# Joined steps for the four tiles of an up-projection group in a one-core encoder layer

## The chip, the cores and the metric

The kernel runs on one core of a Trainium2 chip. The metric is the device time of one execution in microseconds (us); lower is better. Engines are named as in the profile: PE does matrix products, DVE is the vector engine, ACT the scalar (activation) engine, POOL and SP here mostly issue DMA transfers. Each engine runs its own instructions strictly in the order in which they were written for it, and waits at an instruction until the semaphores that it names have been raised.

## What is computed

One encoder layer on 256 positions (T) of 2048 features: a mixer block, then a gated MLP with a convolution over positions, then a final norm. The change lies in the MLP:

```
def conv_ffn(x, g_norm, w_up, conv_k, conv_b, w_down):
    h = rms_norm(x, g_norm)
    up = h @ w_up                                   # (256, 2 * 5504)
    t = up.shape[1]
    pad = jnp.pad(up, ((0, 0), (1, 1), (0, 0)))
    up = (pad[:, :t] * conv_k[0] + pad[:, 1:t + 1] * conv_k[1]
          + pad[:, 2:t + 2] * conv_k[2] + conv_b)
    gate, val = jnp.split(up, 2, axis=-1)
    return x + (jax.nn.silu(gate) * val) @ w_down
```

## The kernel before

**Numbers in two halves.** Products are made of operands that are split into a high and a low half: high times high, low times high, high times low. Weights arrive in *pieces* of 256 rows and up to 512 columns. `split_to` makes the halves of a piece: ACT writes `whi` (line 170), DVE subtracts to get `wlo` (line 171). Four buffers hold `whi` and `wlo`, five hold the raw piece `wraw`.

**The order.** Nothing is scheduled by a program: instructions go out in the order in which the Python code calls them. `begin(i)` opens piece i: it issues the load of piece i+4, then the split of piece i+3 (`split_to(i + SPLIT_AHEAD + 1)`), and then runs the steps that were put at piece i with `at(i, f)`, in the order in which they were put there. So the split of a piece stands in ACT's and DVE's queues behind all steps of the pieces opened earlier.

**The up projection** has 22 groups. A group makes two (the last one: one) tiles of 128 gate channels and as many tiles of value channels, each 128 x 256, from 8 pieces; a full group has 4 PSUM banks, the last one 2. The pieces of the last group have half the columns (128x512 in a split, against 128x1024). `spread_products` issues the high products of two pieces (line 222), then the low products of both (line 226); in a group's last two pieces the high products of the sixteenth 128-row block come behind the low ones.

**Behind a group**, `ev_up(...)` takes its results through these steps: add the two halves of each bank into `ta` (ACT line 1059, DVE line 1061); scale by the norm's factor `rb` (DVE line 1067); middle tap and bias into `tc` (ACT line 1069); the two side taps (DVE lines 1072, 1074); SiLU of the gate (ACT line 1079); gate times value (DVE line 1080); split into the halves of `a`, the left operand of the down projection (ACT line 541, DVE line 542). All but the first run while the pieces of the next group are multiplied: `conv(0)` at its second piece (1 of 0 to 7) with the first gate tile and the first value tile, `conv(1)` two pieces later with the second ones (in the group before last: four pieces later), `gate` and the split one and two pieces behind each. For 13 of the 21 pairs of `a` tiles, sums of blocks are also made (`act_blocks`, lines 323 to 326), split into a tile `so` and written to DRAM by POOL.

**Beside it**, eight jobs (`split_ahead`) load parts of the down weights early into `tw`, add (line 1291), split (ACT line 1296 into the same `so`, DVE line 1297) and write them to DRAM. Each spans two groups: two adds in the last two pieces of the first, two adds and two splits in pieces 0, 1, 2 and 4 of the second.

**The down projection** follows at once: six plain pieces first (lines 317 to 319, twelve products each, the third of them the first to need `wlo`), then pieces in other forms with sums and stored halves that POOL loads into `hpool` and into a pool `twice`. That pool takes the place of the pools of `ta`, `so` and `tw`.

Of the kernel before, what the change touches and what calls it, by code (L numbers as in the profile page):

```python
# [8 lines left out]
F32 = mybir.dt.float32  # L9
BF16 = mybir.dt.bfloat16  # L10
F32R = mybir.dt.float32r
AF = mybir.ActivationFunctionType
OP = mybir.AluOpType
# [3 lines left out]
T = 256  # L17
# [8 lines left out]
NF = DFF // 128  # L26
# [52 lines left out]
def trunk_kernel(ctx, tc, x, x_t, vecs, w_in, ln_g, ln_b, w_st, b_s, rpb, w_branch, w_out, w_up, w_down,  # L79
                 norm_final, out):  # L80
    nc = tc.nc
    ctx.enter_context(tc.manual_schedule())

    def pool(name, side="left", bufs=1, space=None):
        kw = {} if space is None else {"space": space}
        st = ExitStack()
        p = st.enter_context(tc.tile_pool(name=name, bufs=bufs, side=side, reuse_waits="tile", **kw))
        return p, st
# [11 lines left out]
    turns, turns_st = pool("turns")  # L100
    turns = {"p": turns}
# [87 lines left out]
    def at(i, f):  # L189
        tasks.setdefault(i, []).append(f)  # L190

    cur = [0]
# [128 lines left out]
    def act_blocks(w, a11, a21, a12, a22):  # L321
        s3, n1, p2, s4 = (w[:, n * 128:(n + 1) * 128] for n in range(4))
        nc.vector.tensor_sub(s3, a11, a21)
        nc.vector.tensor_sub(n1, a22, a21)
        nc.vector.tensor_add(p2, n1, a11)
        nc.vector.tensor_sub(s4, a12, p2)
# [149 lines left out]
    ck = const.tile([128, 4, 2 * NF], F32)  # L476
# [63 lines left out]
    def split_plain(p, dst):  # L540
        nc.scalar.activation(dst[:, 0, :], p, AF.Copy)
        nc.vector.tensor_sub(dst[:, 1, :], p, dst[:, 0, :].bitcast(F32))
# [26 lines left out]
    def first_room(name, dt):  # L569
        return ypool.tile([128, 2, 512], dt, name=f"y{first_rooms.index('t13' if name == 'f' else name)}")  # L570
# [405 lines left out]
    rs = {}  # L976
# [73 lines left out]
    ff = {}  # L1050

    def ev_up(f0, nb):
        def done(ps, i):
            n = nb
            a = []
            own = {}
            for p in ps:
                t = turns["p"].tile([128, T], F32, name="tb", bufs=3)
                nc.scalar.activation(t, p[:, T:], AF.Copy)
                u = turns["p"].tile([128, T], F32, name="ta", bufs=6)  # L1060
                nc.vector.tensor_add(u, p[:, :T], t)
                a.append(u)

            def conv(b):
                c = []
                for u, ch in ((a[b], f0 + b), (a[n + b], NF + f0 + b)):
                    nc.vector.tensor_mul(u, u, rs["rb"])  # L1067
                    v = ff["p"].tile([128, T], F32, name="tc", bufs=4)
                    nc.scalar.activation(v, u, AF.Identity, scale=ck[:, 1, ch:ch + 1], bias=ck[:, 3, ch:ch + 1])  # L1069
                    c.append((u, v, ch))  # L1070
                for u, v, ch in c:
                    nc.vector.scalar_tensor_tensor(v[:, 1:], u[:, :T - 1], ck[:, 0, ch:ch + 1], v[:, 1:],  # L1072
                                                   op0=OP.mult, op1=OP.add)
                    nc.vector.scalar_tensor_tensor(v[:, :T - 1], u[:, 1:], ck[:, 2, ch:ch + 1], v[:, :T - 1],
                                                   op0=OP.mult, op1=OP.add)
                at(cur[0] + 1, lambda: gate(b, c[0][1], c[1][1]))

            def gate(b, g, v):
                nc.scalar.activation(g, g, AF.Silu)
                nc.vector.tensor_mul(g, g, v)  # L1080
                at(cur[0] + 1, lambda: split_plain(g, ff["a"][f0 + b]))
                own[b] = g
                if b and f0 // 2 in ff["kept"]:
                    at(cur[0] + 2, sums)
                    at(cur[0] + 3, sums_split)

            def sums():
                own["w"] = ff["more"].tile([128, 512], F32, name="sw")
                act_blocks(own["w"], *(own[k][:, t * 128:(t + 1) * 128] for k in range(2) for t in range(2)))

            def sums_split():
                o = ff["more"].tile([128, 2, 512], F32R, name="so")
                split_plain(own["w"], o)
                nc.gpsimd.dma_start(ff["kept"][f0 // 2], o.bitcast(F32))

            at(i + 1, lambda: conv(0))
            if n > 1:
                at(i + (5 if f0 + 3 == NF else 3), lambda: conv(1))
        return done


# [124 lines left out]
    for n, (q, i, j) in enumerate(X_SUMS):  # L1226
        sum_acts_at(i, j, first_sums[2 * q], lambda q=q: q,
                    lambda name, dt, i=i: first_room("s2" if name == "f" and i < 16 else name, dt), f"s{n}", True)
# [97 lines left out]
    for n, (pair, g) in enumerate((pair, g) for g in range(2) for pair in OUT_SPLIT[g]):  # L1326
        t_kept[pair, g] = split_rows("out", pair, g)
        i = g_at[2 * n][1]
# [46 lines left out]
    for n, q in enumerate(OUT_PAIRS):  # L1375
        i = g_m2[0][1] + OUT_SUMS[n]
# [3 lines left out]
    for f in range(0, NF, 2):  # L1380
        nb = min(2, NF - f)
# [27 lines left out]
    for p, turn in zip(DOWN_SPLIT, DOWN_JOBS):  # L1409
        for g in range(2):  # L1410
            d_kept[p, g] = split_rows("down", p, g)
            i = g_up[turn[g]][1]
# [178 lines left out]
```

## Time and profile before

| | |
|---|---|
| Median of 3 runs | 1292.68 us (1291.73 to 1294.64) |
| The profiled execution | 1291.66 us, span of its instructions 1289.9 us |
| PE busy in the span | 1279.3 us (99%) |
| DVE, ACT busy | 1120.4 us (87%), 795.5 us (62%) |
| Up projection on PE | 583.71 to 1064.72 us of the span |
| A full group of it, the last group | 22.27 us, 11.17 us |

Times in a row are from the start of the span. A timeline row gives start, duration, engine, line, operation, output and inputs, how many such instructions follow each other, and the idle time of the engine before it with what ended it. Consecutive instructions of an engine overlap in part: the end of one is later than the start of the next, so what an instruction costs its queue is the distance from its start to the start of the next one, and what it costs one who waits for it is its duration.

### The profile page before, as it was taken

The numbers are of one execution on the slowest core, as the hardware profiler recorded it, in microseconds if no ns is written. First come the engines' busy times: TensorE is split into PE (matmuls) and PEld (weight loads), VectorE is DVE, ScalarE is ACT, GpSimd is POOL, SyncE is SP. The second block draws the span as 40 slices with busy tenths as digits, with TensorE's granted clock in tenths as the row PEclk, the third lists the DMA queues.
The fourth block names the chain that finished last, engine by engine and source line by source line (L and its number), as shares of the span: only waits on it lengthen the run. The fifth ranks groups of instructions, "written<-read, shape, count | busy, mean of one in ns | idle before, by whom it ended". The sixth has DMA issues, their size and how long they took to land.

```text
span 1289.9 us, 19698 instructions
## 1 busy us (share of the span) xinstructions
PE 1279.3 (99%) x6717; PEld 1088.6 (84%) x6717; DVE 1120.4 (87%) x1664; ACT 795.5 (62%) x1181; POOL 169.0 (13%) x307
## 2 busy tenths in 40 slices
PE   9999999999999999999999999999999999999997
PEld 7888888888887888888888888888888888888885
DVE  7898977777789988996889899898988989889987
ACT  7766566766655655566565666566665656655654
POOL 0003706513000001100001001100000001211210
PEclk9999999999999999999999999999999999999999
DMA  9779889899789977965588788888866859998993
GB/s 367 275 277 277 279 273 340 292 325 321 258 309 345 350 240 254 401 222 169 185 290 280 238 291 294 268 270 285 266 221 220 280 171 357 373 390 319 361 384 141
DMA packets 199893, 369.51 MB, mean 286 GB/s; under 512 B 15984, under 2 KB 124144, under 8 KB 199792
## 3 DMA queue, kind: packets, MB, share of 16 engines
q1 hardware_dynamic: 175472, 286.36, 64.8%
q0 software_dynamic: 23888, 81.23, 17.8%
q8 instruction: 52, 0.85, 0.3%
q10 hardware_dynamic: 432, 0.66, 0.1%
q14 instruction: 49, 0.40, 0.1%
HBM read 320.48 MB, written 45.61 MB: 284 GB/s over the span
## 4 chain that ended last, share of the span: by engine, by line
PE 96%; DVE 2%; DMA 1%; issue 1%; DVEq 0%; ACT 0%; SPq 0%; ACTq 0%
PE bank L222 31%; PE bank L226 16%; PE bank L319 11%; PE bank L317 11%; PE bank L318 11%; PE bank L250 5%; PE bank L252 5%; PE bank L251 5%; DVE wlo L171 1%; DMA wraw<-in_w_down_dram 1%; PE bank L867 0%; PE bank L819 0%; PE bank L857 0%; DMA xr<-in_x_t_dram 0%; PE bank L698 0%
## 5 line engine op out<-in xcount | busy, mean ns | idle before, releaser
L171 DVE TENSOR_TENSOR wlo<-wraw,whi 128x1024 fp32r<-128x1024 f32 (+1 forms) x472 | 537.8, 1152 | 124.4 <-ACT whi L170 76.8
L170 ACT ACTIVATE whi<-wraw 128x1024 fp32r<-128x1024 f32 (+1 forms) x472 | 463.6, 995 | 227.1 <-PE bank L318 65.2
L222 PE MATMUL bank<-h,whi 128*128 128x512 f32 x1760 | 423.6, 391 | 0.0
L222 PEld LDWEIGHTS bank<-h,whi 128*128 128x128 f32 x1760 | 322.7, 188 | 62.6 <-issue 0.5
L226 PEld LDWEIGHTS bank<-h,wlo 128*128 128x128 f32 x1760 | 225.9, 191 | 8.7
L226 PE MATMUL bank<-h,wlo 128*128 128x256 f32 x1760 | 228.6, 283 | 0.0
L1069 ACT ACTIVATE tc<-ta,ck 128x256 f32<-128x256 f32 x86 | 47.1, 595 | 110.0 <-DVE ta L1067 110.0
L319 PE MATMUL bank<-wlo,a 128*128 128x512 f32 x188 | 73.4, 390 | 0.2 <-DVE wlo L171 0.2
L317 PE MATMUL bank<-whi,a 128*128 128x512 f32 x188 | 73.2, 389 | 0.0
L318 PE MATMUL bank<-whi,a 128*128 128x512 f32 x188 | 73.2, 389 | 0.0
L319 PE MATMUL bank<-wlo,h 128*128 128x512 f32 x186 | 72.5, 390 | 0.1
L318 PE MATMUL bank<-whi,h 128*128 128x512 f32 x186 | 72.5, 390 | 0.0
L317 PE MATMUL bank<-whi,h 128*128 128x512 f32 x186 | 72.5, 390 | 0.0
L1072 DVE SCALAR_TENSOR_TENSOR tc<-ta,ck,tc 128x255 f32<-128x255 f32 x86 | 41.4, 482 | 14.4 <-ACT tc L1069 14.4
L250 PE MATMUL bank<-whi,y 128*128 128x512 f32 x128 | 50.4, 394 | 0.0
L250 PE MATMUL bank<-whi,h 128*128 128x512 f32 x128 | 50.3, 393 | 0.0
L252 PE MATMUL bank<-wlo,y 128*128 128x512 f32 x128 | 49.8, 389 | 0.0
L252 PE MATMUL bank<-wlo,h 128*128 128x512 f32 x128 | 49.8, 389 | 0.0
L251 PE MATMUL bank<-whi,y 128*128 128x512 f32 x128 | 49.8, 389 | 0.0
L251 PE MATMUL bank<-whi,h 128*128 128x512 f32 x128 | 49.8, 389 | 0.0
L1301 POOL DMA_DIRECT2D down_h<-so x16 | 8.7, 545 | 309.3 <-ACT so L1296 187.2
L374 ACT ACTIVATE h<-h 128x1024 fp32r<-128x1024 f32 x36 | 38.0, 1058 | 13.8 <-DVE h L364 7.1
(324 smaller groups left out, 2005.3 us busy)
## 6 DMA issues: line engine op xcount, KB each, us to landing
wraw<-in_w_up_dram SPq DMA_DIRECT2D x336, 256.0 KB, 4.1
wraw<-in_w_in_dram SPq DMA_DIRECT2D x107, 512.0 KB, 6.6
wraw<-in_w_down_dram SPq DMA_DIRECT2D x78, 512.0 KB, 7.2
wraw<-in_w_in_dram SPq DMA_DIRECT2D x70, 256.0 KB, 4.8
wraw<-in_w_branch_dram SPq DMA_DIRECT2D x32, 512.0 KB, 5.5
wraw<-in_w_out_dram SPq DMA_DIRECT2D x28, 512.0 KB, 5.9
h<-sums POOLq DMA_DIRECT2D x18, 512.0 KB, 7.5
tw<-in_w_down_dram POOLq DMA_DIRECT2D x8, 1024.0 KB, 8.6
```

Of the source, the lines that this page charges most:

```text
L170: nc.scalar.activation(h[:, k, :m], w[:, k, :m], AF.Copy)
L171: nc.vector.tensor_sub(l[:, k, :m], w[:, k, :m], h[:, k, :m].bitcast(F32))
L222: nc.tensor.matmul(p, h[:, k - k0, b * 128:(b + 1) * 128], acts(k), start=k == 0, stop=k == nk - 1)
L226: nc.tensor.matmul(p[:, :T], l[:, k - k0, b * 128:(b + 1) * 128], acts(k)[:, 0, :], start=False, stop=False)
L250: nc.tensor.matmul(p, xh, h[:, kk, :m], start=st, stop=False)
L251: nc.tensor.matmul(p, xl, h[:, kk, :m], start=False, stop=False)
L252: nc.tensor.matmul(p, xh, l[:, kk, :m], start=False, stop=sp)
L317: nc.tensor.matmul(p, xh, h, start=st, stop=False, **kw)
L318: nc.tensor.matmul(p, xl, h, start=False, stop=False, **kw)
L319: nc.tensor.matmul(p, xh, l, start=False, stop=sp, **kw)
L1069: nc.scalar.activation(v, u, AF.Identity, scale=ck[:, 1, ch:ch + 1], bias=ck[:, 3, ch:ch + 1])
L1072: nc.vector.scalar_tensor_tensor(v[:, 1:], u[:, :T - 1], ck[:, 0, ch:ch + 1], v[:, 1:], op0=OP.mult, op1=OP.add)
```

## The change

The four tiles of a group share one `ta` tile (128 x 4 x 256) and one `tc` tile, each with one buffer. Seven steps follow at pieces 1 to 7 of the next group, each in a piece of its own: scaling of all four tiles in one DVE instruction, four middle taps on ACT, eight side taps on DVE (first all left ones, then all right ones), one SiLU, one product, one copy of the high halves, one subtraction of the low halves with the block sums behind it. The split of the block sums follows one and two pieces later, in a tile `sp` of its own.

```
-            at(i + 1, lambda: conv(0))
-            if n > 1:
-                at(i + (5 if f0 + 3 == NF else 3), lambda: conv(1))
+            u = turns["p"].tile([128, 2 * nb, T], F32, name="ta", bufs=1)
+            for n, p in enumerate(ps):
+                nc.scalar.activation(u[:, n], p[:, T:], AF.Copy)
+                nc.vector.tensor_add(u[:, n], p[:, :T], u[:, n])
+            def scale():
+                rb = rs["rb"]
+                nc.vector.tensor_mul(u, u, bass.AP(tensor=rb.tensor, offset=rb.offset,
+                                                   ap=[rb.ap[0], [0, 2 * nb], [1, T]]))
+            def middle():
+                v = box["v"] = ff["p"].tile([128, 2 * nb, T], F32, name="tc", bufs=1)
+                for n, ch in enumerate(channels):
+                    nc.scalar.activation(v[:, n], u[:, n], AF.Identity, scale=ck[:, 1, ch:ch + 1],
+                                         bias=ck[:, 3, ch:ch + 1])
+            def sides():
+                v = box["v"]
+                for tap, to, of in ((0, slice(1, T), slice(0, T - 1)), (2, slice(0, T - 1), slice(1, T))):
+                    for n, ch in enumerate(channels):
+                        nc.vector.scalar_tensor_tensor(v[:, n, to], u[:, n, of], ck[:, tap, ch:ch + 1], v[:, n, to],
+                                                       op0=OP.mult, op1=OP.add)
+            def silu():
+                nc.scalar.activation(v[:, :nb], v[:, :nb], AF.Silu)
+            def gate():
+                nc.vector.tensor_mul(v[:, :nb], v[:, :nb], v[:, nb:])
+            def high():
+                nc.scalar.activation(ff["ap"][f0 // 2][:, :, 0, :], box["v"][:, :nb], AF.Copy)
+            def low():
+                nc.vector.tensor_sub(a[:, :, 1, :], v[:, :nb], a[:, :, 0, :].bitcast(F32))
...
+            def sums_high():
+                box["o"] = ff["more"].tile([128, 2, 512], F32R, name="sp")
...
+            steps = [scale, middle, sides, silu, gate, high, low]
+            if f0 // 2 in ff["kept"]:
+                steps += [sums_high, sums_low]
+            for n, step in enumerate(steps):
+                at(i + 1 + n, step)
```

What that moves is shown at the last group, whose pieces are half as wide. Its pieces are called U0 to U7 here, the first pieces of the down projection D0, D1 and so on; the splits of half a piece show as 128x2x256 below. DVE from the results of the group before last on, in the kernel before (`ta` are the added banks, `tc` the taps, `a_6118` the pair of left operands):

```order
L1061 TENSOR_TENSOR ta<-bank,tb 128x256 x4
L171 TENSOR_TENSOR wlo<-wraw,whi 128x2x256 x2
L1067 TENSOR_TENSOR ta<-ta,rb 128x256 x2
L1072 SCALAR_TENSOR_TENSOR tc<-ta,ck,tc 128x255
L1074 SCALAR_TENSOR_TENSOR tc<-ta,ck,tc 128x255
L1072 SCALAR_TENSOR_TENSOR tc<-ta,ck,tc 128x255
L1074 SCALAR_TENSOR_TENSOR tc<-ta,ck,tc 128x255
L171 TENSOR_TENSOR wlo<-wraw,whi 128x2x256
L1080 TENSOR_TENSOR tc<-tc 128x256
L171 TENSOR_TENSOR wlo<-wraw,whi 128x2x256
L542 TENSOR_TENSOR a_6118<-tc,a_6118 128x256
L171 TENSOR_TENSOR wlo<-wraw,whi 128x2x256
```

The splits are those of U3 and U4, then U5, U6 and U7; four side taps stand between U4 and U5. The same stretch of DVE's order now:

```order
L1057 TENSOR_TENSOR ta<-bank,ta 128x256 x4
L171 TENSOR_TENSOR wlo<-wraw,whi 128x2x256 x2
L1103 TENSOR_TENSOR sp<-sw,sp 128x512
L1063 TENSOR_TENSOR ta<-ta,rb 128x1024
L171 TENSOR_TENSOR wlo<-wraw,whi 128x2x256 x2
L1076 SCALAR_TENSOR_TENSOR tc<-ta,ck,tc 128x255 x8
L171 TENSOR_TENSOR wlo<-wraw,whi 128x2x256
L171 TENSOR_TENSOR wlo<-wraw,whi 128x1024
L1085 TENSOR_TENSOR tc<-tc 128x512
```

All eight side taps now stand between the split of U6 and that of U7, and the split of the block sums (line 1103), which stood ahead of the bank adds, stands behind U4's split. ACT at the same place, before:

```order
L1059 ACTIVATE tb<-bank 128x256 x4
L170 ACTIVATE whi<-wraw 128x2x256 x2
L1069 ACTIVATE tc<-ta,ck 128x256 x2
L170 ACTIVATE whi<-wraw 128x2x256
L1079 ACTIVATE tc<-tc 128x256
L170 ACTIVATE whi<-wraw 128x2x256
L541 ACTIVATE a_6118<-tc 128x256
L170 ACTIVATE whi<-wraw 128x2x256
L170 ACTIVATE whi<-wraw 128x1024
```

The last row is D0. ACT now:

```order
L1056 ACTIVATE ta<-bank 128x256 x4
L170 ACTIVATE whi<-wraw 128x2x256
L1099 ACTIVATE sp<-sw 128x512
L170 ACTIVATE whi<-wraw 128x2x256 x2
L1069 ACTIVATE tc<-ta,ck 128x256 x4
L170 ACTIVATE whi<-wraw 128x2x256 x2
L1081 ACTIVATE tc<-tc 128x512
L170 ACTIVATE whi<-wraw 128x1024 x2
```

The four middle taps stand ahead of U6's high half, and the SiLU, which waits for the side taps on DVE, stands ahead of D0's.

More of the change, by code (lines that the diff above doesn't have):

```diff
@@ L1053, in done @@
         def done(ps, i):
[L1054 to L1089, printed above, removed]
@@ L1091, in sums_split @@
-            def sums_split():
-                o = ff["more"].tile([128, 2, 512], F32R, name="so")
-                split_plain(own["w"], o)
-                nc.gpsimd.dma_start(ff["kept"][f0 // 2], o.bitcast(F32))
-            at(i + 1, lambda: conv(0))
-            if n > 1:
-                at(i + (5 if f0 + 3 == NF else 3), lambda: conv(1))
+            u = turns["p"].tile([128, 2 * nb, T], F32, name="ta", bufs=1)
+            for n, p in enumerate(ps):
+                nc.scalar.activation(u[:, n], p[:, T:], AF.Copy)
+                nc.vector.tensor_add(u[:, n], p[:, :T], u[:, n])
@@ new lines, in done @@
+            box = {}
+            channels = [f + b for f in (f0, NF + f0) for b in range(nb)]
+            def scale():
[7 more added lines that the diff above has]
+                                         bias=ck[:, 3, ch:ch + 1])
@@ new lines, in sides @@
+            def sides():
[5 more added lines that the diff above has]
+            def silu():
+                v = box["v"]
+                nc.scalar.activation(v[:, :nb], v[:, :nb], AF.Silu)
@@ new lines, in gate @@
+            def gate():
+                v = box["v"]
+                nc.vector.tensor_mul(v[:, :nb], v[:, :nb], v[:, nb:])
+            def high():
+                nc.scalar.activation(ff["ap"][f0 // 2][:, :, 0, :], box["v"][:, :nb], AF.Copy)
+            def low():
+                v, a = box["v"], ff["ap"][f0 // 2]
+                nc.vector.tensor_sub(a[:, :, 1, :], v[:, :nb], a[:, :, 0, :].bitcast(F32))
+                if f0 // 2 in ff["kept"]:
+                    box["w"] = ff["more"].tile([128, 512], F32, name="sw")
+                    act_blocks(box["w"], *(v[:, k, t * 128:(t + 1) * 128] for k in range(2) for t in range(2)))
@@ new lines, in sums_high, with sums_low @@
+            def sums_high():
+                box["o"] = ff["more"].tile([128, 2, 512], F32R, name="sp")
+                nc.scalar.activation(box["o"][:, 0], box["w"], AF.Copy)
+            def sums_low():
+                o = box["o"]
+                nc.vector.tensor_sub(o[:, 1], box["w"], o[:, 0].bitcast(F32))
+                nc.gpsimd.dma_start(ff["kept"][f0 // 2], o.bitcast(F32))
+            steps = [scale, middle, sides, silu, gate, high, low]
+            if f0 // 2 in ff["kept"]:
+                steps += [sums_high, sums_low]
```

## The prediction, made before the changed kernel had run

> **What bounds the kernel now.** I read the page's first part, then PE's waits, then the timelines of the last up-projection group, since its pieces give everybody half the time.
>
> ```profile
> PE 1279.3 (99%) x6717; PEld 1088.6 (84%) x6717; DVE 1120.4 (87%) x1664; ACT 795.5 (62%) x1181; POOL 169.0 (13%) x307
> ```
> ```profile
> PE bank L498 <- DVE one L488: 1.5, 1, 1.5
> PE bank L317 <- DVE g L604: 0.8, 1, 0.8
> PE bank L319 <- DVE wlo L171: 0.2, 1, 0.2
> ```
>
> These three waits are all that PE has, and the first two (lines 488 and 604) lie ahead of the up projection. So in the stage that the change touches PE sets the pace alone; work saved on DVE or ACT buys nothing, and the only question is whether some half of a weight now reaches PE too late. The stage by windows, one full group with a job beside it and the last group:
>
> ```profile
> 853.15:875.42 22.27, 22.27 (x129) 19.68 (x128) 20.98 (x36) 13.86 (x21) 2.70 (x5) 1.00 0.81 258
> 1053.55:1064.72 11.17, 11.17 (x66) 9.83 (x64) 9.71 (x20) 6.82 (x15) 1.01 (x2) 1.00 0.81 241
> ```
>
> After the window's length stand the busy times of PE, its weight loads, DVE, ACT and POOL, then the granted clock (1.00) and the DMA share. DVE is busy 20.98 of 22.27 us: it is no bound, but it has little room to catch up. Now PE at the end of the up projection and the start of the down projection:
>
> ```profile
> 1063.30 1.12 PE L226 MATMUL bank<-h,wlo 128*128 128x256 f32 x8
> 1064.25 0.63 PE L222 MATMUL bank<-h,whi 128*128 128x512 f32 x2
> 1064.72 0.39 PE L317 MATMUL bank<-whi,a 128*128 128x512 f32 x1
> 1064.95 0.40 PE L318 MATMUL bank<-whi,a 128*128 128x512 f32 x1
> 1065.18 0.39 PE L319 MATMUL bank<-wlo,a 128*128 128x512 f32 x1
> ```
>
> The eight low products take 0.95 us (1063.30 to 1064.25); the first four are U6's, so U7's `wlo` is due at 1063.78. D0's `whi` is due at 1064.72, its `wlo` 0.46 us later, at 1065.18. DVE before, where it met these dates:
>
> ```profile
> 1049.27 0.29 DVE L323 TENSOR_TENSOR sw<-tc 128x128 f32<-128x128 f32 x1
> ...
> 1051.92 0.69 DVE L171 TENSOR_TENSOR wlo<-wraw,whi 128x512 fp32r<-128x512 f32 x1 [1.51 <-DMA wraw<-in_w_up_dram]
> 1052.53 0.69 DVE L542 TENSOR_TENSOR so<-sw,so 128x512 fp32r<-128x512 f32 x1
> 1053.47 1.42 DVE L1061 TENSOR_TENSOR ta<-bank,tb 128x256 f32<-128x256 f32 x4 [0.26 <-ACT tb L1059]
> 1054.93 0.69 DVE L171 TENSOR_TENSOR wlo<-wraw,whi 128x512 fp32r<-128x512 f32 x1
> ...
> 1058.32 0.48 DVE L1074 SCALAR_TENSOR_TENSOR tc<-ta,ck,tc 128x255 f32<-128x255 f32 x1
> 1058.72 0.48 DVE L1072 SCALAR_TENSOR_TENSOR tc<-ta,ck,tc 128x255 f32<-128x255 f32 x1
> 1059.24 0.48 DVE L1074 SCALAR_TENSOR_TENSOR tc<-ta,ck,tc 128x255 f32<-128x255 f32 x1
> ...
> 1061.66 0.69 DVE L171 TENSOR_TENSOR wlo<-wraw,whi 128x512 fp32r<-128x512 f32 x1
> ```
>
> The last row is U7: done at 1062.35, 1.4 us before PE asks. This is the thinnest cover in the stage, and the change rearranges just this stretch.
>
> **The change, part by part.** *Fewer instructions on DVE.* One 128x1024 and one 128x512 instruction cost their queue, by the next rows (start to start), 1.13 and 0.60 us; a 128x256 one costs 0.34.
>
> ```profile
> 840.29 1.22 DVE L171 TENSOR_TENSOR wlo<-wraw,whi 128x1024 fp32r<-128x1024 f32 x1
> 841.42 0.42 DVE L1080 TENSOR_TENSOR tc<-tc 128x256 f32<-128x256 f32 x1
> 841.76 1.22 DVE L171 TENSOR_TENSOR wlo<-wraw,whi 128x1024 fp32r<-128x1024 f32 x1
> ```
> ```profile
> 853.08 0.68 DVE L1291 TENSOR_TENSOR tw<-tw 128x512 f32<-128x512 f32 x1
> 853.68 0.68 DVE L542 TENSOR_TENSOR so<-sw,so 128x512 fp32r<-128x512 f32 x1
> ```
>
> Per group the scaling falls from 4 x 0.34 = 1.36 to 1.13, product and low halves from 4 x 0.34 to 2 x 0.60: 0.39 us saved. Side taps cost 0.40 where the next is independent (1058.32 to 1058.72) and 0.52 where it needs this one's result (1058.72 to 1059.24). In the new order none needs the one just before it: eight at 0.40 = 3.2 us, against 4 x 0.92 = 3.7. Together about 0.9 us less DVE time in a group, and the waits inside `conv` go too. On PE's path all of it is worth nothing, since no wait of PE in this stage is there to remove: 0.
>
> *The order in full groups.* The side taps stand together, 3.2 us ahead of U7's kind of split. PE in the group from 853.15 on, and DVE's split of its last piece:
>
> ```profile
> 862.35 2.08 PE L226 MATMUL bank<-h,wlo 128*128 128x256 f32 x16
> ```
> ```profile
> 872.58 2.08 PE L226 MATMUL bank<-h,wlo 128*128 128x256 f32 x16
> ```
> ```profile
> 854.28 1.41 DVE L1061 TENSOR_TENSOR ta<-bank,tb 128x256 f32<-128x256 f32 x4
> ...
> 869.67 1.22 DVE L171 TENSOR_TENSOR wlo<-wraw,whi 128x1024 fp32r<-128x1024 f32 x1
> ```
>
> Piece 7's low half is due at 872.58 + 0.95 = 873.53; before, it was there at 870.89. Now: the split of piece 6 needs the buffer of piece 2, which PE frees at about 862.35 + 0.95 + 0.16 = 863.46, and its high half stands behind the four middle taps. The bank adds were over by 855.7; taken 0.5 later, since the block sums now stand just ahead of them, DVE needs from 856.2 on 2 x 1.13 for two splits, 2 x 0.60 for job adds, 0.60 for the block sums' split and 1.13 for the scaling: 861.4. Middle taps then run to 863.5 (beside piece 5's split and the job's on DVE), the high half to 864.6, the split of piece 6 to 865.8, the side taps to 869.1, the split of piece 7 to 870.3. That is 3.2 us early, a little better than before: 0 in 21 groups. If the side taps cost more than 6.4 us, this cover would be gone.
>
> *The last group.* The same order, with half the time. ACT's prices there:
>
> ```profile
> 1057.16 1.09 ACT L1069 ACTIVATE tc<-ta,ck 128x256 f32<-128x256 f32 x2 [1.75 <-DVE ta L1067]
> 1058.16 0.62 ACT L170 ACTIVATE whi<-wraw 128x512 fp32r<-128x512 f32 x1
> ...
> 1065.21 1.04 ACT L170 ACTIVATE whi<-wraw 128x1024 fp32r<-128x1024 f32 x1
> ```
>
> Two middle taps hold ACT 1.00 us, half a piece takes 0.62, a whole piece 1.04. DVE, from U2's split at 1051.92 on, which waits for PE to free a buffer and so does not move: that split 0.61; low halves of the group before (128x512) 0.60; block sums, four at 0.29 at most, 1.1; four bank adds at 0.34, 1.36; these end at 1055.6, 0.7 later than before. U3 and U4 0.61 each, split of the block sums 0.60, scaling 1.13: 1058.55, its result 0.09 later. U5: 1059.2. Meanwhile ACT's four middle taps run from 1058.65 to 1060.65 and U6's high half to 1061.25. DVE: U6 to 1061.9, eight side taps to 1065.1, U7's split (0.69 to its end) to 1065.8. Due at 1063.78: **PE waits 2.0 us.**
>
> *Is that made good later?* D0's high half stands behind the SiLU, which waits for the sixth side tap: 1061.9 + 5 x 0.40 + 0.48 = 1064.4. SiLU of 128x512 is taken as long as U6's copy of that size, 0.6; D0's high half is there at 1066.05 and its low half, 1.22 later, at 1067.3. PE, 2.0 late, asks at 1066.7 and 1067.2: 0.1 more. So even without the wait at U7 a wait of 2.1 us at D0 would stand in its place; the two are one delay, not two. D1's low half (gate product 0.60, split 1.22) is there at 1069.1, due 0.46 after D1's start, which is twelve products or 2.7 us behind D0's: 1070.0. From there on DVE leads again. PE has no idle time to give back until the end, so the sum is **+2.1 us**: 1293.8 us for the profiled execution's 1291.66. That execution is 1.0 below the median of the runs, so against the median 1292.68 + 2.1 = 1294.8 us.
>
> Bounds of that term: side taps at 0.52 each (if the semaphore and not the dependence costs the 0.12) add 1.0 us: 3.1. If the bank adds end as early as before (0.7) and block sums cost 0.2 each (0.4), 1.0. I take the middle, as each step there is a row of the same shape.
>
> [...]
>
> *POOL.* Its loads into `twice` wait for the last reader of the space, now the side taps of the last group, at D3 and not D1. Before:
>
> ```profile
> 1070.66 0.53 POOL L1391 DMA_DIRECT2D s<-sums  x1 [4.95 <-DVE ta L1061]
> 1076.09 0.53 POOL L1251 DMA_DIRECT2D h<-down_h  x1 [4.89 <-ACT whi L170]
> ```
> ```profile
> 1070.00:1075.00 5.00, 5.00 (x24) 4.13 (x23) 4.63 (x9) 3.12 (x6) 0.53 (x1) 1.00 1.03 419
> 1075.00:1080.00 5.00, 5.00 (x24) 4.14 (x23) 4.93 (x9) 3.31 (x6) 2.11 (x4) 1.00 1.02 388
> ```
>
> Following DVE on (bank adds, D3 to D6 and four sums of 0.6), those side taps end near 1081.5; five loads of 0.5 MB then take 2.6 MB / 388 GB/s = 6.8 us alone and perhaps 13 beside the weights: 1094. They are for a piece twelve behind D0 (eight plain ones of 2.7 us, two pairs of 21 products of 0.23 each, so at 1096 before and 1098 now): 0, with 4 us spare.
>
> **The rivals.** *No wait after all* (0.14): DVE or ACT run the last stretch 2 us faster than these rows; the time stays 1292.7. Against it: two separate chains, U7's and D0's, give the same delay. *The delay grows in the down projection* (0.17): transfers there have a DMA share of 1.02 and 1.03, the loads moved from 1071 to 1082 leave the queues idle first and crowd the weights after. If half the 6.8 us is lost as capacity, 3.4, and PE's own 2.1 covers its part, 1.3 more: 1296.1. It decides once those loads land past 1098. *Full groups wait too* (0.05): side taps past 6.4 us; 1 us in each of 8 groups with jobs gives 1303. *DVE is the bound after all* (0.04): the 0.39 us of joined instructions in 21 groups, 8 us, come off: 1284.5. PE's missing waits speak against it. [...]
>
> **The numbers.** The likeliest, a single delay of 1.0 to 3.1 us, has 0.60: 1294.8 us. The range takes in "no wait" and most of the growing delay: 1291.6 to 1297.6, leaving out the last two rivals and the far end of the third. About 0.2% (2.6 us) is what a measurement can tell from no change. A fifth of the likeliest lies over +2.6 (0.12), with 0.15 of the third's and 0.05: slower 0.32. Faster 0.04. Within: 0.64.
>
> **What would show it.** In the profile after: PE's waits name `wlo` of line 171 (or `whi`) once, at about 1063.8, for some 2 us, and no other up-projection piece; eight side taps of 0.40 between U6's and U7's splits; full groups still 22.27 us; DVE busy 15 to 20 us less. Wrong would be: PE without a wait at that place, full groups longer than 22.3 us, or waits on loads past 1080.

## The result, and the profile after

The changed kernel takes 1296.34 us (median of 9 runs, 1294.16 to 1297.00) against 1292.48 us for the kernel before beside it: ratio 1.0027, 95% interval 1.0019 to 1.0036. It is slower by 3.9 us, 0.3%. The profiled execution takes 1294.97 us, with a span of 1292.9 us.

First the page of the changed kernel, then PE's waits in it:

```profile
PE 1280.2 (99%) x6717; PEld 1088.4 (84%) x6717; DVE 1101.7 (85%) x1558; ACT 790.4 (61%) x1139; POOL 168.9 (13%) x307
```
```profile
PE bank L226 <- DVE wlo L171: 1.8, 1, 1.8
PE bank L498 <- DVE one L488: 1.5, 1, 1.5
PE bank L317 <- DVE g L604: 1.2, 1, 1.2
```

DVE is busy 18.7 us less (1120.4 before), and nothing of that shows in the time. One wait is new: low products (line 226) wait for `wlo`, once. The windows of a full group with a job and of the last group:

```profile
854.26:876.53 22.27, 22.27 (x129) 19.68 (x128) 20.80 (x33) 14.91 (x22) 2.65 (x5) 1.00 0.85 276
1054.66:1065.83 11.17, 10.38 (x59) 8.93 (x57) 8.98 (x21) 6.21 (x14) 1.01 (x2) 1.00 0.73 245
```

The full group is as long as before, to the hundredth. The last group, which starts 1.11 us later than before (1054.66 against 1053.55), is not finished after its 11.17 us. DVE and PE at its end, by the timeline:

```profile
1059.56 0.69 DVE L171 TENSOR_TENSOR wlo<-wraw,whi 128x512 fp32r<-128x512 f32 x1
1062.38 0.69 DVE L171 TENSOR_TENSOR wlo<-wraw,whi 128x512 fp32r<-128x512 f32 x1 [2.12 <-ACT whi L170]
1062.99 3.24 DVE L1076 SCALAR_TENSOR_TENSOR tc<-ta,ck,tc 128x255 f32<-128x255 f32 x8
1066.14 0.68 DVE L171 TENSOR_TENSOR wlo<-wraw,whi 128x512 fp32r<-128x512 f32 x1
1067.14 1.23 DVE L171 TENSOR_TENSOR wlo<-wraw,whi 128x1024 fp32r<-128x1024 f32 x1 [0.31 <-ACT whi L170]
```
```profile
1064.41 0.63 PE L226 MATMUL bank<-h,wlo 128*128 128x256 f32 x4
1066.88 0.74 PE L226 MATMUL bank<-h,wlo 128*128 128x256 f32 x4 [1.84 <-DVE wlo L171]
1067.46 0.62 PE L222 MATMUL bank<-h,whi 128*128 128x512 f32 x2
1067.92 0.39 PE L317 MATMUL bank<-whi,a 128*128 128x512 f32 x1
1068.15 0.39 PE L318 MATMUL bank<-whi,a 128*128 128x512 f32 x1
1068.42 0.50 PE L319 MATMUL bank<-wlo,a 128*128 128x512 f32 x1
```

The splits are U5, U6, U7 and D0; the eight side taps stand between U6 and U7. Four low products start 0.12 us apart, so U7's first was to start at 1064.41 + 4 x 0.12 = 1064.88; it starts at 1066.88: **2.0 us late**. The last row is D0's first use of `wlo`, 0.27 instead of 0.23 us behind its neighbour: 0.04 us more, and no second wait. Behind it PE never waits again.

The span is 3.0 us longer than that of before, and 1.1 of it lie ahead of the change, where the up projection starts later. Its first high products in the kernel before, in the changed kernel, and in a second profile of the kernel before (run later, below):

```profile
583.71 1.75 PE L222 MATMUL bank<-h,whi 128*128 128x512 f32 x7
```
```profile
584.81 0.62 PE L222 MATMUL bank<-h,whi 128*128 128x512 f32 x2
```
```profile
584.70 0.84 PE L222 MATMUL bank<-h,whi 128*128 128x512 f32 x3
```

The unchanged kernel starts there at 584.70 too. So that 1.1 us needs no change of the kernel: it is scatter between executions, and the first profile of before was a quick one.

### The profile page after: what moved, and what is told of

Same layout as the page of the kernel before. It is cut to its first block, busy times and chain, and to the rows that moved or that the text cites. A ratio compares the mean times of both kernels' runs of the same rounds, so it can differ in the third digit from the quotient of the medians.

```text
span 1292.9 us, 19590 instructions
## 1 busy us (share of the span) xinstructions
PE 1280.2 (99%) x6717; PEld 1088.4 (84%) x6717; DVE 1101.7 (85%) x1558; ACT 790.4 (61%) x1139; POOL 168.9 (13%) x307
## 4 chain that ended last, share of the span: by engine, by line
PE 96%; DVE 2%; DMA 1%; issue 0%; ACT 0%; DVEq 0%; ACTq 0%
PE bank L222 31%; PE bank L226 16%; PE bank L319 11%; PE bank L317 11%; PE bank L318 11%; PE bank L250 5%; PE bank L252 4%; PE bank L251 4%; DMA wraw<-in_w_in_dram 1%; DVE wlo L171 1%; PE bank L867 0%; PE bank L819 0%; PE bank L857 0%; DMA xr<-in_x_t_dram 0%; PE bank L698 0%
## 5 line engine op out<-in xcount | busy, mean ns | idle before, releaser
L1076 DVE SCALAR_TENSOR_TENSOR tc<-ta,ck,tc 128x255 f32<-128x255 f32 x172 | 69.8, 480 | 0.0
L785 POOL TENSOR_SCALAR_AFFINE_SELECT bias<-run 64x128 f32<-64x128 f32 x64 | 36.6, 605 | 81.2 <-DVE sc L827 80.6
```

What stands on the lines that cost most here:

```text
L1076: nc.vector.scalar_tensor_tensor(v[:, n, to], u[:, n, of], ck[:, tap, ch:ch + 1], v[:, n, to], op0=OP.mult, op1=OP.add)
```

## The experiments

"Joined" means the steps as the change writes them, "spread" those of before.

**The changed kernel again** (no edit).

> The changed kernel once more, as the yardstick of the other three. Theory A (one delay: U7's low half behind eight side taps, D0's high half behind the SiLU): the trace shows one PE wait in the up projection, 2.0 us before the low products of U7, and the time is 2 us over before (ratio 1.0016). Rival B (joined steps cost a second thing that this wait does not hold, for instance the later POOL loads into `twice` or the full groups): 3 to 5 us over before again (1.0023 to 1.0039), with 1 to 3 us that no PE wait in the last group explains.

Measured: 1295.57 us (8 runs, 1294.56 to 1297.19) against 1292.17; ratio 1.0028, interval 1.0017 to 1.0038. The loss is real, 3.4 us this time. Its profile has the same 2.0 us wait, and one thing more, which the last section shows.

**Spread steps only behind the group before last**, joined ones in the other twenty-one.

```
-            for n, step in enumerate(steps):
-                at(i + 1 + n, step)
+            if f0 + 3 != NF:
+                for n, step in enumerate(steps):
+                    at(i + 1 + n, step)
+                return
...
+            at(i + 1, lambda: conv(0))
+            at(i + 5, lambda: conv(1))
```

> Joined steps in every group but the one before last, whose two pairs of tiles go through the old steps in the old pieces (on the shared tiles); POOL's loads into `twice` still wait for the side taps of the last group. Theory A: no PE wait over 0.3 us after line 604's; ratio 1.000 within its interval; U7's low half 1.0 to 1.5 us early. Rival B: the rest of the loss stays, 1 to 3 us over before (1.0008 to 1.0023).

Measured: 1293.42 us; ratio 1.0010, 1.0001 to 1.0019. The wait at U7 is gone, and two thirds of the loss with it. A smaller one stands at D1, in PE's timeline of this kernel:

```profile
1068.45 0.39 PE L318 MATMUL bank<-whi,a 128*128 128x512 f32 x1
1069.39 0.50 PE L319 MATMUL bank<-wlo,a 128*128 128x512 f32 x1 [0.56 <-DVE wlo L171]
```

D1's `wlo` comes 0.94 instead of 0.23 us behind: 0.7 us. The group ahead of it still has joined steps, so the split of its block sums (0.60 us on DVE) still stands behind the bank adds. PE's waits on `wlo` in this run count one more: at 1274.88, near the end of the down projection, a product comes 0.66 us late, where the kernel before has 0.36.

**The reverse: joined steps only behind the group before last**, spread ones elsewhere, with the block sums' split at its old place.

```
-            for n, step in enumerate(steps):
-                at(i + 1 + n, step)
+            if f0 + 3 == NF:
+                for n, step in enumerate(steps):
+                    at(i + 1 + n, step)
+                return
...
```

> The opposite: old steps in the old pieces in every group (on the shared tiles), joined steps only behind the group before last. The split of the block sums stands ahead of the bank adds again, so DVE comes to the scaling 1.3 us earlier than in the changed kernel. Theory A: one PE wait before U7's low products, 2.0 - 1.3 = 0.7 to 0.8 us, and a time 0.8 us over before (ratio 1.0006). Rival B (the loss comes from the 20 other groups): no more than 0.3 us. A rival C (the joined order in the last group is harmless, its length does it): 2 us.

Measured: 1294.30 us; ratio 1.0015, 1.0007 to 1.0024. The wait is back at U7, from these steps alone, though smaller:

```profile
1063.80 0.63 PE L226 MATMUL bank<-h,wlo 128*128 128x256 f32 x4
1065.62 0.74 PE L226 MATMUL bank<-h,wlo 128*128 128x256 f32 x4 [1.18 <-DVE wlo L171]
```

1065.62 - (1063.80 + 0.48) = 1.34 us; I had expected 0.7 to 0.8. So of the 2.0 us, 1.34 come from the joined steps of this one group; by difference, 0.66 come from the joined steps of the group ahead of it, which put the block sums and their split later. I had taken off the whole 1.3 us that these cost DVE. About half of that is lost, because DVE, so much earlier here, waits before U4's split until PE frees a buffer:

```profile
1056.61 0.69 DVE L171 TENSOR_TENSOR wlo<-wraw,whi 128x512 fp32r<-128x512 f32 x1 [0.53 <-PE bank L226]
```

The time is 2.1 us over before, 0.8 more than the wait; that part stays open.

**The joined steps of the group before last three pieces later.**

```
-                at(i + 1 + n, step)
+                at(i + (4 if f0 + 3 == NF else 1) + n, step)
```

> The changed kernel with the seven joined steps of the group before last three pieces later (scaling at U4, side taps at U6, SiLU at U7, product at D0, and so on); no other edit and no less work. Theory A: now the splits of U7, D0 and D1 stand ahead of the side taps and those of D2 on behind, where pieces last 2.7 us; no PE wait over 0.3 us, D2's low half 0.7 us early, ratio 1.000. Rival B: 1 to 3 us over before (1.0008 to 1.0023). If the amount of joined work in the last group counted and not what it stands ahead of, it would wait 2 us as before.

Measured: 1294.24 us; ratio 1.0017, 1.0008 to 1.0026. No wait at U7 or from D0 to D6; but one at D7, which I had not expected:

```profile
1083.05 0.39 PE L318 MATMUL bank<-whi,a 128*128 128x512 f32 x1
1084.70 0.50 PE L319 MATMUL bank<-wlo,a 128*128 128x512 f32 x1 [1.26 <-DVE wlo L171]
```

It is 1.65 - 0.23 = 1.4 us long. DVE in that kernel shows why:

```profile
1078.71 0.69 DVE L171 TENSOR_TENSOR wlo<-wraw,whi 128x512 fp32r<-128x512 f32 x1 [1.74 <-ACT whi L170]
1079.32 0.69 DVE L363 TENSOR_TENSOR h<-wraw 128x512 f32<-128x512 f32 x1
...
1081.85 1.66 DVE L1076 SCALAR_TENSOR_TENSOR tc<-ta,ck,tc 128x255 f32<-128x255 f32 x4
1083.43 1.22 DVE L171 TENSOR_TENSOR wlo<-wraw,whi 128x1024 fp32r<-128x1024 f32 x1
```

Steps moved out of one full stretch of DVE's queue pushed the next one: the last group's side taps and four weight sums now end just when D7's split is due.

**No side taps behind the group before last.**

```
             def sides():
                 v = box["v"]
+                if f0 + 3 == NF:
+                    return
```

> The changed kernel without the eight side taps of the group before last (its gate values are computed without them; 3.2 us of VectorE work, nothing else). Theory A (the whole loss is PE waiting at U7 for the split behind these taps): U7's `wlo` is ready 3.2 us earlier, so the 2.0 us wait is gone, none stands in its place at D0 to D7, and the time is that of before, ratio 0.9990 to 1.0010. Theory B (part of the loss is elsewhere: the timed 3.1 to 3.9 us are more than the 2.0 us wait): the waits are gone and 1 to 2 us remain, ratio 1.0008 to 1.0016.

Measured: 1292.35 us against 1292.40; ratio 0.9998, 0.9989 to 1.0007. Theory A. With 3.2 us of DVE work out of one place, no other change undone, all of the loss is gone, so it hangs on this one wait; twenty groups of joined steps cost and save nothing that this interval (some 1.2 us to each side) can show. DVE's splits of U6 and U7 now follow each other, and U7's is done at 1063.94:

```profile
1062.65 1.29 DVE L171 TENSOR_TENSOR wlo<-wraw,whi 128x512 fp32r<-128x512 f32 x2 [2.13 <-ACT whi L170]
```

**Later steps again, with the last group's side taps ahead of the weight sums.**

```
                 v = box["v"] = ff["p"].tile([128, 2 * nb, T], F32,
-                    name="tc", bufs=1)
+                    name="tc" if nb > 1 else "tl", bufs=1)
...
+            if nb == 1:
+                steps[:2] = [lambda: (scale(), middle())]
             for n, step in enumerate(steps):
-                at(i + 1 + n, step)
+                at(i + (4 if f0 + 3 == NF else 1) + n, step)
```

> The changed kernel with the group before last started three pieces later, as in the run before this one, and the last group's scaling and middle taps in one step, so that its side taps come a piece earlier and stand ahead of the weight sums, not between them and D7's split (its middle taps get a tile of their own). Theory A (position in VectorE's queue decides): no wait at U7, D0 to D2, nor at D7 (1.65 us before): no PE wait in this stage, ratio 0.9990 to 1.0008. Rival (the VectorE work itself is too much for this stretch wherever it stands): a wait of 0.5 to 1.5 us appears at another down piece, ratio 1.0008 to 1.0018.

Measured: 1294.43 us; ratio 1.0015, 1.0006 to 1.0024. Theory A's forecast of no wait fails: D7 waits 1.8 us, not less than before. The rows of ACT and DVE of this kernel:

```profile
1074.71 1.09 ACT L1069 ACTIVATE tl<-ta,ck 128x256 f32<-128x256 f32 x2 [1.10 <-DVE ta L1063]
1075.71 1.56 ACT L170 ACTIVATE whi<-wraw 128x1024 fp32r<-128x1024 f32 x2
```
```profile
1076.79 1.23 DVE L171 TENSOR_TENSOR wlo<-wraw,whi 128x1024 fp32r<-128x1024 f32 x1 [2.12 <-ACT whi L170]
```

The middle taps, a piece earlier, now stand ahead of a high half on ACT (1075.71), and DVE, which stands at that piece's split, waits 2.1 us with the side taps behind it. I had moved the work past DVE's obstacle and into ACT's. The rival, too much work wherever it stands, forecast another piece and a ratio of 1.0008 to 1.0018. The ratio lies there, but the wait is at D7 as before and DVE had 2.1 us idle, so the amount of its work is not the reason.

**How long is the cover in a full group?** Two runs, with 8 and with 16 further side taps (3.2 and 6.4 us) in three groups that are not neighbours, whose gate values change by them; the factor 2 is 3 in the second. In the first profile after, where no job stands ahead, DVE's split of a group's last piece (the first of two here) and the low products that need it:

```profile
847.26 2.36 DVE L171 TENSOR_TENSOR wlo<-wraw,whi 128x1024 fp32r<-128x1024 f32 x2
```
```profile
851.42 2.08 PE L226 MATMUL bank<-h,wlo 128*128 128x256 f32 x16
```

It is ready at 847.26 + 1.22 = 848.48 and due 0.95 behind the second row's start, at 852.37: a cover of 3.9 us.

```
-                for tap, to, of in ((0, ...), (2, ...)):
+                for tap, to, of in ((0, ...), (2, ...)) * (2 if f0 in (20, 28, 36) else 1):
```

> The changed kernel with eight further side taps (3.2 us of VectorE; the gate values of these groups change) in three full groups that are not neighbours. In the trace of the changed kernel piece 7's low half is ready 3.9 us ahead of PE in such groups. Theory A (cover): 3.2 is less than 3.9, so PE does not wait and these groups still take 22.27 us. Rival (VectorE's busy time counts): each of the three groups becomes longer by up to 3.2 us less its idle 2.4 to 2.9 us, 0.3 to 0.8 each.

> The same with sixteen further side taps (6.4 us of VectorE) in the same three groups. Theory A (cover): PE waits 6.4 - 3.9 = 2.5 us for `wlo` once in each of the three groups, 7.5 us in all, besides the 2.0 us at U7. Rival (buffers further ahead make it good): no wait, or under 1 us in each. Rival (busy time counts): 6.4 - 2.4 to 2.9 = 3.5 to 4.0 us in each.

Measured with 8 (one run of each): 1294.87 us, and no wait in the up projection but the one at U7. With 16: 1303.12 us, and one wait in each of the three groups. PE's waits of that kernel, and the first of them:

```profile
PE bank L226 <- DVE wlo L171: 8.9, 4, 2.4
```
```profile
851.74 0.28 PE L226 MATMUL bank<-h,wlo 128*128 128x256 f32 x1
854.34 0.86 PE L226 MATMUL bank<-h,wlo 128*128 128x256 f32 x5 [2.32 <-DVE wlo L171]
```

2.60 us between two starts that are otherwise 0.12 apart: 2.5 us, as the cover of 3.9 us said (6.4 - 3.9), and nothing at 3.2. By busy time it would have been 3.5 to 4.0 us in each group, and 0.3 to 0.8 with 8. In such a group the distance of one split from its date decides.

**Spread steps behind the group before last, and the block sums a piece earlier.**

```
             if f0 // 2 in ff["kept"]:
                 steps += [sums_high, sums_low]
+            if f0 + 5 == NF:
+                steps[4:6] = [lambda: (gate(), high())]
```

(on top of the second experiment)

> The earlier kernel with the old spread steps in the group before last, and besides the product and the high half of the group ahead of it in one piece, so that its low half, block sums and their split come a piece earlier, into a stretch where VectorE is idle for 2.3 us (1050.4 to 1052.7 us there), and no longer ahead of the splits of U5 to D1. All other groups have the joined steps. Theory A (position in VectorE's queue decides): D1's `wlo`, 0.7 us late there, is in time; no PE wait from U0 to D7; ratio 0.9990 to 1.0007. Rival (joined steps in the other twenty groups cost something that no wait shows, about the 0.0010 of the earlier kernel): the wait goes and the ratio stays at 1.0008 to 1.0015.

Measured: 1292.52 us against 1292.56; ratio 1.0001, 0.9992 to 1.0011. D1's low products, 0.7 us late in the second experiment, are 0.1 us late here:

```profile
1067.89 0.39 PE L318 MATMUL bank<-whi,a 128*128 128x512 f32 x1
1068.23 0.50 PE L319 MATMUL bank<-wlo,a 128*128 128x512 f32 x1
```

Joined steps in twenty-one groups cost nothing that this interval can show; this version computes all of the reference and is as quick as the kernel before, not quicker.

**The kernel before once more.**

> The kernel before once more, for the wait at line 604 ahead of the up projection, whose gap between two matmul starts was 1.19 us in its first profile and 1.61 to 1.74 us in the nine of the changed kernels. Theory A (scatter between runs, nothing of the change): 1.6 to 1.7 us here too, or anything between. Rival (the change does it, by other places in memory): 1.19 us again. Time 1291.3 to 1293.4 us either way.

Measured: 1292.73 us. PE's waits have the one at line 604 at 1.2 us, as the changed kernels had; the kernel of the experiment above, with joined steps in twenty-one groups, has it at 0.4:

```profile
PE bank L317 <- DVE g L604: 1.2, 1, 1.2
```
```profile
PE bank L317 <- DVE g L604: 0.4, 1, 0.4
```

So it varies in both kernels: it is scatter. Against this profiled execution the changed kernel's is 2.24 us longer (1294.97 to 1292.73), which is the wait at U7 and hardly more.

## Why the prediction was right, and where it was not

*The place and the size of the wait* were right. Forecast: U7's `wlo` 2.0 us late, behind eight side taps of 0.40. Measured: 2.0 us, and eight in 3.24 us. The steps of its chain hold too: moved by the 1.11 us of the later start, it had U7's split done at 1065.8 + 1.1 = 1066.9; the row says 1066.14 + 0.68 = 1066.82.

*One delay, not two.* D0's SiLU chain was to add 0.1 us; it adds 0.04. D0's low half was done at 1067.14 + 1.23 = 1068.37, 0.05 us before PE used it at 1068.42; had PE not waited at U7, it would have asked 2.0 us earlier and waited as long there. That is worked out from the rows: no run takes the two chains apart, since without side taps the SiLU comes earlier too.

*Full groups cost nothing.* Forecast: piece 7's low half ready 3.2 us early in a group with a job. In the profile after:

```profile
870.13 1.22 DVE L171 TENSOR_TENSOR wlo<-wraw,whi 128x1024 fp32r<-128x1024 f32 x1
```
```profile
873.69 2.08 PE L226 MATMUL bank<-h,wlo 128*128 128x256 f32 x16
```

Ready at 871.35, due 0.95 behind the second row's start, at 874.64: 3.3 us. The limit that the prediction gave there, 3.2 us more, was not tried; the two runs with further side taps bracket the 3.9 us of groups where no job stands ahead. So the rivals that full groups wait and that DVE is the bound both fall; DVE lost 18.7 us of work and PE none.

*POOL.* The loads into `twice` did come later, the first at 1083.15 instead of 1070.66:

```profile
1083.15 0.53 POOL L1403 DMA_DIRECT2D s<-sums  x1 [14.23 <-ACT tc L1081]
```

PE has no wait behind U7 in its list, and the first product that uses one of these tiles starts at 1100.74 (1098 in the prediction), so they land in time and the rival of a growing delay falls too. PE even had a little to give back, against the prediction: the product at 1273.17 in the kernel before comes 0.36 us late, its counterpart 0.07. The last group's side taps ended at 1082.6, not at 1081.5 as reckoned, which still left room.

*The step that failed* is the last: that the delay in a profile is the delay in the median. Forecast +2.1 and 1294.8 us; the median is +3.4 and +3.9 in two comparisons, 1.3 to 1.8 more, which puts the result among "slower by over 0.2%", where I had given 0.32, and not "within", 0.64. The range held it. A part of the excess goes with a lower granted clock (last section), for which the sum has no term. In nine of the seventeen runs of the changed kernel the mean granted clock is 0.996 or 0.997, and their median is 1296.34 us; the eight at 0.998 have 1295.1, which is 1.2 us less. Of the thirty runs of the kernel before beside the second comparison none is below 0.998. The rest is 0.6 to 0.9 us: without the lower clock the changed kernel is still 2.6 to 3.0 us over before, for a delay of 2.04. It stays open. The two kernels with a wait of 1.3 to 1.4 us have it too: they took 2.1 us more, without a lower clock.

The spread steps remove the wait at U7 (2.0 to 0 us). But the eight side taps are eight instructions in both kernels; what the spread steps change there is who stands between them, not their length. Whether joining helps a DVE that is the bound, no run here shows, because DVE at 85 to 87% was not.

## What to carry to other kernels

Work joined on DVE, which kept the order of its queue here (2.1 us idle at a split with the side taps behind it), was paid for not by its own length but by whoever stood behind it. Before joining, list what is queued behind, the date at which each is due, and compare the joined block with the thinnest of these covers. The thinnest is found where the rhythm changes, here at a last group with half the time; the joined steps can stand in all others. Moving such a block later, or ahead, paid here only where the stretch that it moved into had room on every engine that its steps touch: two of three moves (steps later, side taps ahead, block sums earlier) brought the wait back elsewhere (1.4 and 1.8 us at D7).

## What the hardware showed that I had not expected

The PE wait of 2.0 us at U7 cost more than 2.0 us in two of the four profiles that have it (1.8 to 1.9 us of idle PE): there PE runs at half clock behind it, 0.50 in the window of 2 us that lies whole in such a stretch (1076.00 to 1078.00, below). The repeat of the changed kernel:

```profile
1066.24 1.07 PE L226 MATMUL bank<-h,wlo 128*128 128x256 f32 x4 [1.84 <-DVE wlo L171]
1067.10 1.05 PE L222 MATMUL bank<-h,whi 128*128 128x512 f32 x2
1067.96 0.63 PE L317 MATMUL bank<-whi,a 128*128 128x512 f32 x1
1068.38 0.63 PE L318 MATMUL bank<-whi,a 128*128 128x512 f32 x1
```

The products start 0.43 us apart, not 0.23 as in the rows of the first profile after. The windows of the same stretch, first in that repeat, then in the first profile (after the length stand PE's busy time and the granted clock):

```profile
1066.00:1068.00 2.00, 1.76 (x7) 0.61 0.76 260
1068.00:1070.00 2.00, 2.00 (x7) 0.54 0.74 223
```
```profile
1066.00:1068.00 2.00, 1.12 (x7) 1.00 0.79 250
1068.00:1070.00 2.00, 2.00 (x10) 1.00 0.75 207
```

Six products at 0.43 cost 1.2 us there, and 1.4 with the slower ones beside them; in the run with 16 further side taps eight cost 1.5 us behind U7. Yet the three waits of 2.5 us in that run's full groups were followed by full clock (1.00), and so were the other two at U7. The windows of that run behind the second of the three, and behind U7:

```profile
946.00:948.00 2.00, 1.97 (x12) 1.00 0.34 96
1074.00:1076.00 2.00, 1.82 (x7) 0.66 0.76 236
1076.00:1078.00 2.00, 2.00 (x6) 0.50 0.81 227
```

Two microseconds at a granted clock of 0.61 hold 1.56 us of half clock, and at 0.54 they hold 1.84: in the repeat it lasts about 3.4 us, by this estimate from its two windows. In the first profile after, half clock shows only at the very end, where PE has no work left (its last product starts at 1284.47), and the repeat has it there too (1284.94). First the repeat, then the first profile after:

```profile
1288.00:1289.00 1.00, 0.00 (x0) 0.66 0.96 352
```
```profile
1288.00:1289.00 1.00, 0.00 (x0) 0.80 0.98 367
```

What decides which wait has half clock behind it is not shown. The length of the wait alone does not: 1.84 us of idle PE at U7 had it behind them in the repeat and not in the first profile after, and of the seven waits of 1.8 us and more in the four profiles the three longest, with 2.3 to 2.4 us of idle PE, did not have it. No run moved a wait to try it. Over all runs, a mean clock below 0.998 stands in nine of seventeen runs of the changed kernel, but in one of 66 of the kernel before and in one of 66 of the six variants timed several times, in whose profiles the longest such wait leaves PE idle for 1.62 us.

My estimate from these profiles: a wait of about two microseconds on PE is best priced here with a range that reaches 1.5 us past its length (half clock cost 1.2 to 1.5 us where it came), and one of 1.62 us or less without it.
